# Attention with tokens on partitions in the output: four heads are divided by their sums at once and transposed back

## The chip, the cores and the metric

The kernel runs on one core of a Trainium2 chip. The metric is the device time of one execution in microseconds. The kernel before has a median of 1493.06 us over three runs (1490.69 to 1493.82).

## The reference

Two transformer blocks for 256 tokens of width 1024, in float32. The first block mixes tokens in four ways (FoX attention, a gated delta rule, HGRN and GLA) and ends in a gated feed-forward layer; the second has two attentions of eight heads (MoBA and MLA), gates, and a layer of 16384 experts. The change concerns the three attentions, all causal, with heads of 64 value columns. Each computes for a head

```
s = einsum('bhqd,bhkd->bhqk', q, k) * scale        # FoX adds c[q] - c[k]; MLA has a rotary part
s = where(k_pos <= q_pos, s, -inf)
p = softmax(s)
o = einsum('bhqk,bhkd->bhqd', p, v)
```

With 256 tokens MoBA has one block of keys, so it is plain causal attention. FoX has four heads, MoBA and MLA eight each.

## The kernel before, in words

Activations lie with features on partitions and the 256 tokens along the free axis. Weights come from HBM by SP's queue as 128x1024 float32 tiles; ScalarE copies each into a rounded `hi` (line 163, carried out in the helper at line 146) and VectorE or GpSimd subtracts to get `lo` (line 164), and a projection makes three matmuls of each pair of tiles (`dense_n`, line 314; `columns_into`, line 364; `branch`, lines 178 to 180). `prefetch` issues these for the weight after next.

The attentions share the generator `attention` (line 937). For head i, `soft` writes the scores into one PSUM bank: queries 0 to 127 against 128 keys, queries 128 to 255 against 256 keys (lines 1178 and 1179 for FoX, 1543 for MoBA, 1555 and 1556 for MLA). VectorE adds the mask and takes the maxima (lines 946 and 948), scales the maxima (line 950), ScalarE makes the exponentials and their sums, and VectorE takes the reciprocal of the sums (line 953) and scales the two parts (lines 954 and 955). One turn later the three 128x128 pieces are transposed (line 974) and ScalarE copies them to SBUF as `at_t` (`fat` in FoX). Another turn later `pv` multiplies: the values are stationary (128 keys x 64 columns), the transposed probabilities move (256 and 128 columns, lines 933 and 934), and the output has features on partitions, two heads above each other. A bank holds four heads. When the fourth is done, `after` (line 1526) has ScalarE copy the bank to `yos`, and `split` (line 182) makes the `hi` and `lo` for the output projection; FoX copies its bank to `os_` and goes on to its norm (`finish`, line 906: squares, a matmul at line 492, the reciprocal root).

Float32 matmuls show up as two passes each; a transpose is one.

The order of the work is written out by hand. Every stage is a Python generator, and the strings `TURNS1` and `TURNS2` say which of them emits its next piece (`follow`, line 387). Each engine carries out its instructions in the order of emission. A projection emits half a tile at a turn, 12 matmuls. Around the ends of the groups of four heads the order is:

- FoX: fourth product, then 24 projection matmuls with two weight splits, then the step that copies the bank and squares it, then the split of another mixer's output (`Xh` from `gatez`, `Xl`), then the norm's matmul.
- MoBA, heads 0 to 3: fourth product, scores of head 5, 24 projection matmuls with one weight split on VectorE, then the step, which goes on with the transposes of head 4.
- MoBA, heads 4 to 7: fourth product, 36 projection matmuls and other work, the scores of an MLA head, 12 projection matmuls, the step.
- MLA, heads 0 to 3: fourth product, scores of head 5, the step at once, with the transposes of head 4 behind it, 12 projection matmuls, the product of head 4.
- MLA, heads 4 to 7: fourth product, the step at once, then the output branch of MLA, the first half of whose matmuls needs heads 0 to 3 only.

PSUM has eight banks: four under the tag "m" (scores, transposes, norms), two "n" (outputs of MoBA and MLA), two "d" (projections).

Of the kernel before, what the change touches and what calls it, by code (L numbers as in the profile page):

```python
# [116 lines left out]
def _emit(ctx, tc, I, out):  # L117
# [819 lines left out]
    def attention(pool, heads, scores, scale, v, out_of, new_e, new_t, tag, after=lambda h: None,  # L937
                  names=lambda h: (), lt=1, lp=1):
        sc, pt = {}, {}

        def soft(i):
            b = bank(tag)
            scores(heads[i], b)
            e = new_e(i)
            m = pool.tile([128, 4], F32, tag="at_m", name="at_m", bufs=4)
# [4 lines left out]
            V.tensor_scalar(m[:, 0:2], m[:, 0:2], -scale, None, op0=OP.mult)  # L950
            A(e[:, 0:128], e[:, 0:128], AF.Exp, bias=m[:, 0:1], scale=scale, accum_out=m[:, 2:3])
            A(e[:, 128:384], e[:, 128:384], AF.Exp, bias=m[:, 1:2], scale=scale, accum_out=m[:, 3:4])
            V.reciprocal(m[:, 2:4], m[:, 2:4])
            V.tensor_scalar(e[:, 0:128], e[:, 0:128], m[:, 2:3], None, op0=OP.mult)
            V.tensor_scalar(e[:, 128:384], e[:, 128:384], m[:, 3:4], None, op0=OP.mult)
            sc[i] = e

        n = len(heads)
        for i in range(n + lt + lp):
            j = i - lt - lp  # L960
            if j >= 0:
                t = pt.pop(j)
                pv(out_of(heads[j]), t[:, 0:256], t[:, 256:384], lambda kt: v(kt, heads[j]))
            if i < n:
                yield from need(*names(heads[i]))
                soft(i)
            yield
            if j >= 0:
                after(heads[j])
            if 0 <= i - lt < n:  # L970
                b = bank(tag)
                e = sc.pop(i - lt)
                for z in range(3):
                    PE.transpose(b[:, z * 128:(z + 1) * 128], e[:, z * 128:(z + 1) * 128], ident)
                pt[i - lt] = new_t(i - lt)
                A(pt[i - lt], b[:, :384], AF.Copy)
                yield
# [169 lines left out]
    def fox():  # L1147
# [26 lines left out]
        def scores(h, b):  # L1174
            r_ = slice((h % 2) * 64, (h % 2) * 64 + 64)
            for w, t, n in ((b[:, 0:128], 0, 128), (b[:, 128:384], 1, 256)):
# [4 lines left out]
        o = bank()  # L1181
        ab_ = [z.rearrange("p (a b) -> p a b", a=2) for z in (mp.tile([128, 768], F32, tag="ffb", name="fae"), mp.tile([128, 768], F32, name="fat"))]
        yield from attention(tmp, range(4), scores, 1.0, lambda kt, h: vcols(kt, h * 64),
                             lambda h: head(b2(o), h), lambda i: ab_[0][:, i % 2], lambda i: ab_[1][:, i % 2], "m")
        os_ = q
        A(os_, b2(o), AF.Copy)
        yield from finish(0, os_, "fon", None, "m")

    follow([main1(), gdn(), fox(), hgrn(), gla(), gdn_gates()], TURNS1)
# [325 lines left out]
                              out_rows(3), branch("b", 3), out_rows(4), out_rows(5), out_rows(6), out_rows(7)])  # L1515

    def attend(n, scores, scale, v, names=lambda h: ()):
        o = {}

        def out_of(h):  # L1520
            g = h // 4
            if g not in o:
                o[g] = b2(bank("n"))
            return o[g][(h % 2) * 64:(h % 2) * 64 + 64, (h % 4) // 2]

        def after(h):
            if h % 4 == 3:
                g = h // 4
                os_ = btmp.tile([128, 2, 256], F32, tag="yos", name="yos")
                A(os_, o[g], AF.Copy)  # L1530
                split(os_, ya[n][0][:, 2 * g:2 * g + 2], ya[n][1][:, 2 * g:2 * g + 2])

        yield from attention(btmp, range(8), scores, scale, lambda kt, h: v[:, kt, h * 64:h * 64 + 64], out_of,
                             lambda i: btmp.tile([128, 384], F32, tag="at_e" + n, name="at_e", bufs=LAG[0] + 1),
                             lambda i: btmp.tile([128, 384], F32, tag="at_t" + n, name="at_t", bufs=LAG[1] + 1), "m", after, names, *LAG)

    def moba():
        def scores(h, b):
# [475 lines left out]
```

## Time and profile before

| what | us |
|---|---|
| median of three runs | 1493.06 |
| the profiled execution's own time | 1492.48 |
| its span, first to last instruction | 1490.5 |
| TensorE matmul busy | 1430.4 (96%) |
| VectorE busy | 1011.9 (68%) |
| ScalarE busy | 778.6 (52%) |
| GpSimd busy | 293.3 (20%) |
| mean granted TensorE clock | 0.978 of full speed |

Times in a profile count from the start of the span. PE is TensorE's matmuls and PEld its weight loads, DVE is VectorE, ACT ScalarE, POOL GpSimd, SP the engine that issues most DMAs. A row of the timeline gives the start, the time from there to the end of the last instruction merged into the row, the engine, the line, the operation, what it writes and reads, its shape (for a matmul the stationary operand first, as 128*64 for 128 rows and 64 columns, then the moving one), how many were merged, and in brackets how long the engine had been idle and what ended that. Helpers record their own line: all of ScalarE's activations stand at L146. Successive matmuls overlap, so the time of one is read from the start of the next.

### The profile page before, as it was taken

The page shows a single profiled execution, that of the slowest core. Times are in us where ns is not written, and L with a number is a line of the kernel's source. Part 1 is how long each engine was busy: PE and PEld are TensorE (multiplying, and loading weights), DVE is VectorE, ACT ScalarE, POOL GpSimd, SP SyncE. Part 2 cuts the span into 40 slices and gives each one's busy share as a digit, 9 for nine tenths or more (in the row PEclk, how much of TensorE's full clock was granted, in tenths as well). Part 3 has the DMA queues.
Part 4 walks back from the last instruction along what each step waited for, and adds up shares of the span by engine and source line. Part 5 has one row for each costly group of instructions (what it writes and reads, how often), then busy time and mean ns, then how long its engine had stood idle before and what let it go on. Part 6 is the DMA issues. An engine that isn't in the chain of part 4 may idle for free.

```text
span 1490.5 us, 27184 instructions
## 1 busy us (share of the span) xinstructions
PE 1430.4 (96%) x11076; PEld 1305.4 (88%) x11076; DVE 1011.9 (68%) x1846; ACT 778.6 (52%) x1068; POOL 293.3 (20%) x133
## 2 busy tenths in 40 slices
PE   8699989999999899999999999999999999999998
PEld 7588858999998678799999999788889999978886
DVE  5577757997786645467998887666663333666665
ACT  5633435566564446444556666444445555654444
POOL 1000000000002115332670000000037777700000
PEclk9899979999999989999999999999999999999999
DMA  6322203456654223354565455566665555566664
GB/s 235 114 85 76 68 15 116 167 192 196 185 173 155 89 93 116 111 175 151 157 190 178 156 156 157 182 193 192 194 188 168 169 170 170 171 189 194 197 194 131
DMA packets 63791, 231.42 MB, mean 155 GB/s; under 512 B 7073, under 2 KB 7602, under 8 KB 63282
## 3 DMA queue, kind: packets, MB, share of 16 engines
q1 hardware_dynamic: 62640, 226.00, 48.5%
q10 hardware_dynamic: 1026, 3.68, 0.8%
q8 instruction: 87, 1.43, 0.4%
q14 instruction: 38, 0.31, 0.1%
HBM read 228.60 MB, written 1.05 MB: 154 GB/s over the span
## 4 chain that ended last, share of the span: by engine, by line
PE 85%; DVE 8%; ACT 4%; issue 2%; DMA 0%; SPq 0%; DVEq 0%; ACTq 0%
PE bd L314 36%; PE bm L1833 8%; PE bm L1834 8%; PE bm L1832 8%; PE bn L314 6%; PE bm L348 5%; PE bn L1785 2%; DVE lo L164 2%; PE bacc L364 1%; PE bd L376 1%; ACT hi L146 1%; PE bn L933 1%; PE bm L1543 1%; PE bn L1059 1%; PE bm L1556 1%
## 5 line engine op out<-in xcount | busy, mean ns | idle before, releaser
L146 ACT ACTIVATE hi<-raw 128x1024 fp32r<-128x1024 f32 x426 | 448.1, 1057 | 180.3 <-PE bm L1833 54.3
L164 DVE TENSOR_TENSOR lo<-raw,hi 128x1024 fp32r<-128x1024 f32 x310 | 381.1, 1235 | 144.8 <-ACT hi L146 144.8
L164 POOL TENSOR_TENSOR lo<-raw,hi 128x1024 fp32r<-128x1024 f32 x116 | 284.0, 2464 | 846.6 <-ACT hi L146 557.0
L314 PE MATMUL bd<-Xh,hi 128*128 128x256 f32 x1560 | 392.6, 290 | 9.3 <-ACT hi L146 7.1
L314 PE MATMUL bd<-Xl,hi 128*128 128x256 f32 x1560 | 381.9, 283 | 0.0
L314 PEld LDWEIGHTS bd<-Xh,hi 128*128 128x128 f32 x1560 | 296.4, 190 | 14.4 <-ACT hi L146 10.2
L314 PEld LDWEIGHTS bd<-Xl,hi 128*128 128x128 f32 x1560 | 296.6, 190 | 0.8 <-issue 0.2
L314 PE MATMUL bd<-Xh,lo 128*128 128x256 f32 x1560 | 216.2, 281 | 0.0
L1832 PE MATMUL bm<-hi,eh 128*128 128x512 f32 x512 | 199.4, 389 | 2.9 <-ACT eh L146 2.9
L1833 PE MATMUL bm<-hi,el 128*128 128x512 f32 x512 | 199.4, 389 | 0.5 <-DVE el L184 0.5
L1834 PE MATMUL bm<-lo,eh 128*128 128x512 f32 x512 | 199.2, 389 | 0.0
L314 PEld LDWEIGHTS bd<-Xh,lo 128*128 128x128 f32 x1560 | 198.5, 188 | 0.0
L1770 DVE TENSOR_TENSOR oi<-iorow,IT 128x1024 f16<-128x1024 f16 x64 | 59.4, 929 | 114.3 <-PE bn L1785 112.3
L146 ACT ACTIVATE Gt<-bn 128x512 f32<-128x512 f32 x64 | 71.3, 1114 | 116.4 <-PE bn L1785 116.4
L1832 PEld LDWEIGHTS bm<-hi,eh 128*128 128x128 f32 x512 | 96.1, 188 | 23.2 <-ACT eh L146 3.3
L1833 PEld LDWEIGHTS bm<-hi,el 128*128 128x128 f32 x512 | 96.1, 188 | 20.8 <-DVE el L184 1.1
L1834 PEld LDWEIGHTS bm<-lo,eh 128*128 128x128 f32 x512 | 96.1, 188 | 20.0
L146 ACT ACTIVATE eh<-act 128x512 fp32r<-128x512 f32 x64 | 40.4, 632 | 118.8 <-DVE act L1813 118.8
L184 DVE TENSOR_TENSOR el<-act,eh 128x512 fp32r<-128x512 f32 x64 | 44.3, 692 | 49.4 <-ACT eh L146 49.4
L1772 DVE TENSOR_TENSOR jg<-eqj,GHL 128x1024 f16<-128x1024 f16 x64 | 50.7, 792 | 2.2
L314 PE MATMUL bn<-Xl,hi 128*128 128x256 f32 x192 | 47.7, 286 | 0.6 <-DVE Xl L251 0.6
L314 PE MATMUL bn<-Xh,hi 128*128 128x256 f32 x192 | 47.1, 282 | 0.0
(588 smaller groups left out, 2067.9 us busy)
## 6 DMA issues: line engine op xcount, KB each, us to landing
raw<-in_eu SPq DMA_DIRECT2D x128, 512.0 KB, 3.6
raw<-in_ev SPq DMA_DIRECT2D x128, 512.0 KB, 3.8
raw<-in_w_in SPq DMA_DIRECT2D x61, 512.0 KB, 3.6
raw<-in_w_up SPq DMA_DIRECT2D x44, 512.0 KB, 3.9
raw<-in_w_down SPq DMA_DIRECT2D x22, 512.0 KB, 4.2
raw<-in_w_out SPq DMA_DIRECT2D x16, 512.0 KB, 3.5
raw<-in_w_query SPq DMA_DIRECT2D x16, 512.0 KB, 4.0
raw<-in_w_ba SPq DMA_DIRECT2D x4, 512.0 KB, 3.5
```

The lines of the kernel that those rows point to most:

```text
L146: S.activation(o, i, f, **kw)
L164: (V if by == "v" else G).tensor_tensor(lo[:, :width], raw[:, :width], hi[:, :width].bitcast(F32), op=OP.subtract)
L184: V.tensor_tensor(lo, src, hi.bitcast(F32), op=OP.subtract)
L314: PE.matmul(o, w[:, k * 128:k * 128 + M], x[:, k], start=n == 0, stop=n == 23)
L348: PE.matmul(acc[n // 2][:, (n % 2) * 256:(n % 2) * 256 + 256], w[:, n * 128:n * 128 + 128], x, start=first and n % 2 == 0 and w is ws[0][0 ...
L364: PE.matmul(acc[n // 2][:, (n % 2) * 256:(n % 2) * 256 + 256], w[:, i * 512 + n * 128:i * 512 + n * 128 + 128], x, start=first and n % 2 = ...
L1770: V.tensor_tensor(oi, along(64), pairs(IT[:, ts], 64), op=OP.is_equal)
L1772: V.tensor_tensor(jg.rearrange("p (t i) j e -> p t i (j e)", i=2), eq.rearrange("p t j e -> p t (j e)")[:, :, None].to_broadcast([128, 8, ...
L1785: PE.matmul(p[:, t, :nj], oi[:, t].rearrange("p a b -> p (a b)"), jg[:, 2 * t + i].rearrange("p a b -> p (a b)"), start=i == 0, stop=i == 1)
L1832: PE.matmul(o, eh[:, i, ts], v[0][:, n_], start=False, stop=False, skip_group_check=True)
L1833: PE.matmul(o, el[:, i, ts], v[0][:, n_], start=False, stop=False, skip_group_check=True)
L1834: PE.matmul(o, eh[:, i, ts], v[1][:, n_], start=False, stop=last and j + i == nj - 1, skip_group_check=True)
```

## The change

The probabilities stay unscaled: line 953's reciprocal and the two scalings leave the head. The sums of four heads are gathered in one tile. The product has the transposed, unscaled probabilities stationary (128x128) and the values moving (64 columns), in three matmuls, so that the output has tokens on partitions and four heads side by side in one bank. After the fourth head, VectorE takes the reciprocal of all eight columns of sums, multiplies the bank by it into `z`, TensorE transposes `z` in four pieces into a fresh bank of tag "m", and `split` (FoX: the copy to `os_`) reads that bank directly; the copy to `yos` is gone. FoX's output bank is taken when the first product is made, and its `z` lies in the memory of the keys.

```diff
-            V.reciprocal(m[:, 2:4], m[:, 2:4])
-            V.tensor_scalar(e[:, 0:128], e[:, 0:128], m[:, 2:3], None, op0=OP.mult)
-            V.tensor_scalar(e[:, 128:384], e[:, 128:384], m[:, 3:4], None, op0=OP.mult)
+            A(e[:, 0:128], e[:, 0:128], AF.Exp, bias=m[:, 0:1], scale=scale, accum_out=tot[g][:, 0, c:c + 1])
+            A(e[:, 128:384], e[:, 128:384], AF.Exp, bias=m[:, 1:2], scale=scale, accum_out=tot[g][:, 1, c:c + 1])
             sc[i] = e
+
+        def group(g):
+
+            r = tot.pop(g)
+            V.reciprocal(r, r)
+            z = new_z()
+            V.tensor_tensor(z, out.pop(g), r[:, :, :, None].to_broadcast([128, 2, 4, 64]), op=OP.mult)
+            b = bank(tag)
+            for t in range(2):
+                for hp in range(2):
+                    PE.transpose(b[:, hp * 256 + t * 128:hp * 256 + t * 128 + 128],
+                                 z[:, t, 2 * hp:2 * hp + 2].rearrange("p a b -> p (a b)"), ident)
+            return b2(b)
...
-                t = pt.pop(j)
-                pv(out_of(heads[j]), t[:, 0:256], t[:, 256:384], lambda kt: v(kt, heads[j]))
+                p = pt.pop(j)
+                g, c = divmod(j, 4)
+                if c == 0:
+                    out[g] = bank(otag).rearrange("p (t h d) -> p t h d", t=2, h=4)
+                o = out[g]
+                PE.matmul(o[:, 0, c], p[:, 0:128], v(0, heads[j]), start=True, stop=True, skip_group_check=True)
+                PE.matmul(o[:, 1, c], p[:, 128:256], v(0, heads[j]), start=True, stop=False, skip_group_check=True)
+                PE.matmul(o[:, 1, c], p[:, 256:384], v(1, heads[j]), start=False, stop=True, skip_group_check=True)
...
-            if j >= 0:
-                after(heads[j])
+            if j >= 0 and j % 4 == 3:
+                whole(j // 4, group(j // 4))
...
-        os_ = q
-        A(os_, b2(o), AF.Copy)
+                             lambda: k.rearrange("p a (b d) -> p a b d", b=4), "m", "m",
+                             lambda g, o: A(os_, o, AF.Copy))
...
-                os_ = btmp.tile([128, 2, 256], F32, tag="yos", name="yos")
-                A(os_, o[g], AF.Copy)
-                split(os_, ya[n][0][:, 2 * g:2 * g + 2], ya[n][1][:, 2 * g:2 * g + 2])
+                             lambda: btmp.tile([128, 2, 4, 64], F32, tag="at_z", name="at_z"), "m", "n",
+                             lambda g, o: split(o, ya[n][0][:, 2 * g:2 * g + 2], ya[n][1][:, 2 * g:2 * g + 2]), names, *LAG)
```

The turns and their strings are the same.

## Rows read from the trace of the kernel before

**Rows 1.** The page: busy time and instructions by engine; the chain by engine.
```profile
PE 1430.4 (96%) x11076; PEld 1305.4 (88%) x11076; DVE 1011.9 (68%) x1846; ACT 778.6 (52%) x1068; POOL 293.3 (20%) x133
...
PE 85%; DVE 8%; ACT 4%; issue 2%; DMA 0%; SPq 0%; DVEq 0%; ACTq 0%
```

**Rows 2.** Busy time by stretch: length, PE, PEld, DVE, ACT, POOL, granted clock, DMA.
```profile
548.00:551.00 3.00, 3.00 (x9) 1.48 (x8) 1.20 (x8) 0.98 (x4) 0.00 (x0) 0.50 0.11 38
551.00:554.00 3.00, 3.00 (x7) 1.47 (x8) 0.44 (x3) 0.00 (x0) 0.00 (x0) 0.50 0.00 0
554.00:557.00 3.00, 3.00 (x15) 3.00 (x16) 1.88 (x9) 0.99 (x4) 0.00 (x0) 0.51 0.00 0
...
605.00:608.00 3.00, 3.00 (x9) 1.68 (x8) 0.58 (x4) 1.29 (x2) 2.11 (x1) 0.50 0.00 0
608.00:611.00 3.00, 3.00 (x16) 3.00 (x15) 1.55 (x7) 2.60 (x7) 0.31 (x1) 0.50 0.50 180
```

**Rows 3.** Groups by line and shape, 470 to 640 us: busy, mean ns, idle before.
```profile
L955 DVE TENSOR_SCALAR at_e<-at_e,at_m 128x256 f32<-128x256 f32 x16 | 5.6, 348 | 0.0
...
L953 DVE RECIPROCAL at_m<-at_m 128x2 f32<-128x2 f32 x16 | 2.7, 166 | 17.0 <-ACT at_e L146 17.0
...
L1458 DVE TENSOR_TENSOR gta<-bd,R 128x512 f32<-128x512 f32 x4 | 2.7, 683 | 0.0
```

**Rows 4.** Timeline, FoX: its first head, its last product and its norm.
```profile
197.16 2.08 PE L492 MATMUL bn<-hsq,cst 128*128 128x512 f32 x2
...
199.82 0.68 DVE L234 TENSOR_SCALAR f3v<-bn 128x512 f32<-128x512 f32 x1
...
233.23 0.60 ACT L146 ACTIVATE fq<-bm 128x512 f32<-128x512 f32 x1 [0.56 <-PE bm L934]
...
234.01 2.35 DVE L164 TENSOR_TENSOR lo<-raw,hi 128x1024 fp32r<-128x1024 f32 x2
...
236.07 1.02 PE L492 MATMUL bm<-hsq,cst 128*128 128x512 f32 x2
...
245.10 0.38 PE L364 MATMUL bacc<-Xl,hi 128*128 128x256 f32 x1 [1.82 <-DVE Xl L184]
```

**Rows 5.** Timeline, MLA: the product of a head and the scores after it.
```profile
583.53 0.65 PE L933 MATMUL bn<-at_t,vb 128*64 128x256 f32 x2
...
584.33 0.48 PE L1555 MATMUL bm<-kno,qno 64*128 64x128 f32 x2
...
584.74 0.48 PE L1556 MATMUL bm<-kpe,qpe 32*128 32x128 f32 x2
```

**Rows 6.** Timeline: float32 matmuls with 128x128 stationary and few moving columns.
```profile
126.03 0.28 PE L683 MATMUL bm<-g,cst 128*128 128x4 f32 x2
...
127.73 0.31 PE L717 MATMUL bm<-kept,s 128*128 128x128 f32 x1
...
725.03 2.01 PE L1627 MATMUL bm<-keys,qT 128*128 128x128 f32 x16
```

**Rows 7.** Timeline, MoBA, the step after its fourth head.
```profile
534.00 0.49 PE L974 MATMUL bm<-kept,at_e 128*128 128x128 f32 x3
534.02 1.23 DVE L164 TENSOR_TENSOR lo<-raw,hi 128x1024 fp32r<-128x1024 f32 x1 [0.20 <-ACT hi L146]
```

**Rows 8.** Timeline, MoBA, ahead of the step after its eighth head.
```profile
572.44 0.17 DVE L950 TENSOR_SCALAR at_m<-at_m 128x2 f32<-128x2 f32 x1
...
573.17 0.28 PE L314 MATMUL bd<-Xh,hi 128*128 128x256 f32 x1
```

**Rows 9.** Timeline, MLA, around the step after its fourth head.
```profile
599.74 0.55 PE L974 MATMUL bm<-kept,at_e 128*128 128x128 f32 x3
...
600.52 0.17 DVE L950 TENSOR_SCALAR at_m<-at_m 128x2 f32<-128x2 f32 x1
...
603.28 0.43 PE L933 MATMUL bn<-at_t,vb 128*64 128x256 f32 x1 [1.58 <-ACT at_t L146]
```

**Rows 10.** Timeline, MLA, the output branch after its eighth head.
```profile
631.59 0.38 PE L178 MATMUL bd<-yb,hi 128*128 128x256 f32 x1 [0.44 <-ACT yb L146]
```

More of the change, by code (lines that the diff above doesn't have):

```diff
@@ L934, in pv, with attention @@
         PE.matmul(o[:, 128:256], v(1), pt1, start=False, stop=True, skip_group_check=True)
-    def attention(pool, heads, scores, scale, v, out_of, new_e, new_t, tag, after=lambda h: None,
-                  names=lambda h: (), lt=1, lp=1):
-        sc, pt = {}, {}
+    def attention(pool, heads, scores, scale, v, new_e, new_t, new_z, tag, otag, whole, names=lambda h: (), lt=1, lp=1):
+        sc, pt, out, tot = {}, {}, {}, {}
         def soft(i):
+            g, c = divmod(i, 4)
+            if c == 0:
+                tot[g] = pool.tile([128, 2, 4], F32, tag="at_s", name="at_s", bufs=2)
             b = bank(tag)
@@ L944, in soft @@
             e = new_e(i)
-            m = pool.tile([128, 4], F32, tag="at_m", name="at_m", bufs=4)
+            m = pool.tile([128, 2], F32, tag="at_m", name="at_m", bufs=4)
             V.tensor_tensor_reduce(out=e[:, 0:128], in0=b[:, 0:128], in1=mask[:, 128:256], op0=OP.add, op1=OP.max,
@@ L961, in attention @@
             if j >= 0:
-                t = pt.pop(j)
-                pv(out_of(heads[j]), t[:, 0:256], t[:, 256:384], lambda kt: v(kt, heads[j]))
+                p = pt.pop(j)
+                g, c = divmod(j, 4)
+                if c == 0:
+                    out[g] = bank(otag).rearrange("p (t h d) -> p t h d", t=2, h=4)
[3 more added lines that the diff above has]
+                PE.matmul(o[:, 1, c], p[:, 256:384], v(1, heads[j]), start=False, stop=True, skip_group_check=True)
             if i < n:
@@ L1179, in scores @@
                 PE.matmul(w, ca[r8, ts], cb[r8, h, 0:n], start=False, stop=True)
-        o = bank()
+        os_ = q
         ab_ = [z.rearrange("p (a b) -> p a b", a=2) for z in (mp.tile([128, 768], F32, tag="ffb", name="fae"), mp.tile([128, 768], F32, name="fat"))]
         yield from attention(tmp, range(4), scores, 1.0, lambda kt, h: vcols(kt, h * 64),
-                             lambda h: head(b2(o), h), lambda i: ab_[0][:, i % 2], lambda i: ab_[1][:, i % 2], "m")
-        os_ = q
-        A(os_, b2(o), AF.Copy)
+                             lambda i: ab_[0][:, i % 2], lambda i: ab_[1][:, i % 2],
+                             lambda: k.rearrange("p a (b d) -> p a b d", b=4), "m", "m",
+                             lambda g, o: A(os_, o, AF.Copy))
         yield from finish(0, os_, "fon", None, "m")
@@ L1517, in attend @@
     def attend(n, scores, scale, v, names=lambda h: ()):
[L1518 to L1528, printed above, removed]
-                os_ = btmp.tile([128, 2, 256], F32, tag="yos", name="yos")
-                A(os_, o[g], AF.Copy)
-                split(os_, ya[n][0][:, 2 * g:2 * g + 2], ya[n][1][:, 2 * g:2 * g + 2])
-        yield from attention(btmp, range(8), scores, scale, lambda kt, h: v[:, kt, h * 64:h * 64 + 64], out_of,
+        yield from attention(btmp, range(8), scores, scale, lambda kt, h: v[:, kt, h * 64:h * 64 + 64],
                              lambda i: btmp.tile([128, 384], F32, tag="at_e" + n, name="at_e", bufs=LAG[0] + 1),
-                             lambda i: btmp.tile([128, 384], F32, tag="at_t" + n, name="at_t", bufs=LAG[1] + 1), "m", after, names, *LAG)
+                             lambda i: btmp.tile([128, 384], F32, tag="at_t" + n, name="at_t", bufs=LAG[1] + 1),
+                             lambda: btmp.tile([128, 2, 4, 64], F32, tag="at_z", name="at_z"), "m", "n",
+                             lambda g, o: split(o, ya[n][0][:, 2 * g:2 * g + 2], ya[n][1][:, 2 * g:2 * g + 2]), names, *LAG)
     def moba():
```

4 lines of the change are left out of this document (1 added, 3 removed).

## The prediction

> **What bounds the kernel now.** I read the page first, then the busy time by stretch, then the groups of the attention stretches by shape, then the timeline around each place where a group of four heads ends. TensorE is the bound: 1430 us of a 1490.5 us span, and 85% of the chain that ended last [rows 1]. So a microsecond of matrix work, or of TensorE standing still, counts nearly in full; a microsecond of VectorE counts only where TensorE waits for it. The attentions run near 193 to 245 us (FoX) and 473 to 632 us (MoBA, MLA), woven into the projections. There TensorE counts as busy 3.00 us of every 3, yet the granted clock falls to 0.50, that is 1.2 of its 2.4 GHz [rows 2]; the work in the two low stretches is scores, products and transposes, the long projections being the minority. Half speed over 548 to 557 costs some 4.5 us (1.5 + 1.5 + 1.47), over 605 to 611 some 3.0.
>
> **VectorE, removed per head.** A reciprocal (0.17 us) and two scalings (0.35 for the wide one, the narrow one no more): some 0.8 us, twenty times, 16 us in all [rows 3]. The reciprocal also holds VectorE about 1.06 us for the exponentials (17.0 us over 16 heads). I cost this gain at nothing in MoBA and MLA. What follows there in VectorE's queue is mostly a weight split `lo`, which waits for ScalarE's `hi`, and that stands behind the same exponentials; so the queue stalls on `hi` instead of on the sums. TensorE's list of waits has none of a transpose of probabilities on the scalings. If that cover is gone, at most the 16 us less what runs beside matmuls would come back; no row shows it. In FoX the chain does pass through the scalings. Their successor starts at 199.82, while its input, a matmul begun at 197.16 and 2.08 long, is there at 199.24 [rows 4]: **-0.6 us**; bounds 0 and, were both blocked heads to gain the whole 0.8, -1.6.
>
> **The products.** Before: two matmuls a head, each two passes, 64 stationary columns, 256 and 128 moving; from 583.53 to the next work at 584.33 that is 0.80 us [rows 5]. After: three matmuls, six passes, 128 stationary columns and 64 moving. No row has that shape, but two bracket it [rows 6]: with 4 moving columns 16 passes took 126.03 to 127.73, 0.106 each; with 128 moving, 16 passes lasted 2.01 in all, at most 0.126. I take 0.11, as the shape lies between them: 0.66 a head, -0.14 by twenty heads, **-2.8 us**. The low end is 0.106 (-3.3). The high end is from the scores, whose matmul with 128 moving columns took 0.41 (584.33 to 584.74) [rows 5]: 0.21 of it two loads, the rest the stream, so with half the stream 0.31 a matmul, 0.93 a head, +2.6.
>
> **The five group ends.** Each now has, in one step: the sums' reciprocal (0.17), one multiply of 128x512 out of PSUM (0.69 as the projection evictions [rows 3]), four transposes (4 x 0.11 = 0.44), then the copy or split. The multiply waits for the fourth product, and the transposes for the multiply. TensorE is in order, so everything behind stands still: projection matmuls, the next head's transposes. I place each by the order in which the instructions stand now.
>
> *FoX.* The group's step comes after 24 projection matmuls, and VectorE is in two `lo` splits until 234.01 + 2.35 = 236.36 [rows 4]. Reciprocal and multiply end near 237.2, the transposes 237.9; the copy (0.60, until now at 233.23 under those matmuls) and a square taken as long now follow, and the norm's matmul starts at 239.2 in place of 236.07. ScalarE's `Xh` of the gated output stood behind the square, so it slides too, and its `Xl` after it, ahead of the norm on VectorE: the chain loses some 3.4. Nothing absorbs it, for the end of that chain, `Xl` at 245.1, is what TensorE already waits 1.82 for: **+3.4 us**.
>
> *MoBA, first group.* The transposes would stand where a head's transposes start now, 534.00; a `lo` split ahead of the reciprocal starts at 534.02 and takes 1.23 [rows 7]. z is ready at 536.1: a stall of 2.1, plus 0.44: **+2.5**. Behind the stalled step wait ScalarE's split of the result, the next `at_t` copy, a `hi`, and on VectorE the projection's eviction; all slide by about as much as TensorE does, so no second wait follows.
>
> *MoBA, second.* VectorE ends the next head's maximum at 572.61; z at about 573.6; the 12 matmuls before the step end at 573.17 [rows 8]: 0.43 + 0.44, **+0.9**.
>
> *MLA, first.* No other work lies between scores and step: TensorE would stand from 599.74 until z, 600.69 + 0.17 + 0.69 and gaps, 601.65 [rows 9]. But today it waits 1.58 for `at_t`, since two ScalarE copies stand ahead; one is gone, and that wait is eaten. After the four transposes (0.44), the three (0.3) and 12 matmuls (1.45) the product starts at 603.9 in place of 603.28: **+0.6**.
>
> *MLA, second.* The copy (0.60, as FoX's) becomes the multiply (0.69) and the transposes with their drain (0.6); the half of the first output branch that needs no new data still covers the split. The second half, now at 631.59 after a wait of 0.44 [rows 10], starts some 0.7 later: **+0.7**.
>
> The four removed ScalarE copies count nothing beyond that. No DMA is added or moved, so SP's queue is the same, and POOL's instructions stand as before; their `lo` splits only start later with TensorE. The extra PSUM bank rotates among four, freed in each case earlier than it is asked for again: nothing, bounds 0 to +0.5 a group.
>
> **Sum.** -0.6 - 2.8 + 3.4 + 2.5 + 0.9 + 0.6 + 0.7 = +4.7 on the profiled execution, 1492.48, gives 1497.2. The median of the runs is 0.6 above that execution, so I forecast 1497.8 for the median.
>
> **Rivals.** *A, the forecast*, 0.46; alone 1495.3 to 1500.3.
>
> *B, the products cost more than the bracket* (load and stream in series, as in the scores): +5.4 over my value, 1503.2. For it: scores do so in the same stretch. Against: they use part of the rows, and both bracketing rows use the full array. 0.08.
>
> *C, the clock falls once more.* The stalls at 534 and 599 are each followed by transposes and short products; a new low stretch like that at 605 to 611 costs 3.0, one like 548 to 557 4.5: 1500.8 to 1502.3. For it: today's low stretch at 605 begins after the 1.58 wait [rows 2, 9]. Against: dense projections follow most stalls. 0.14. Of that the Trainium skill says (TensorE: Matmul & The Clock Gate, Part 4: PE-mode transpose) that transposes do not count as busy for the clock gate in the way matmuls do. By that rule the 20 added transposes lengthen each idle patch and C would be the forecast, 1500.8 in place of 1497.8. The trace neither shows nor denies it, since its low stretches mix transposes with scores and products.
>
> *D, the clock stays up.* Full-width products replace half-width ones just where the clock is low now; if both low stretches go, 7.5 is given back: 1490.3, not slower than before. It decides from the point where the clock holds through 548 to 557. For it: the products there are the only half-width work. Against: the scores, with 32 or 64 rows, remain and are longer. 0.20.
>
> *E, the stalls are covered.* If VectorE, freed of 16 us, reaches the multiplies early, what is left is transposes (+2.2), products (-2.8) and FoX's -0.6, with half of FoX's tail (+1.7): +0.5, 1493.6. Against: in each place I named the instruction in front of the reciprocal, and none of them is removed. 0.12.
>
> **Numbers.** 0.2%, about 3 us, is what a measurement of this kernel can tell from no change: faster is below 1490.1, slower above 1496.0. A gives 0.40 slower and 0.06 same; B and C 0.22 slower; D 0.09 faster and 0.11 same; E 0.10 same and 0.02 faster. So faster 0.11, same 0.27, slower 0.62. The range 1489.5 to 1503 reaches from D's lower half to the dearer C and the edge of B.
>
> **What would show it.** Right: TensorE waiting on VectorE's z for some 2 us in MoBA's first and MLA's first group and 0.4 in MoBA's second; FoX's norm matmul about 3 us later after its last product; a head's products at 0.66; MoBA's and MLA's weight splits no earlier against the exponentials. Wrong: no waits on z; products at 0.9; TensorE's clock at full through MoBA's last heads; or a low clock behind the new stalls. A gain of over 3 us would mean that VectorE's relief or the clock, which I leave out of the forecast, did the work.

## The result and the profile after

The changed kernel takes **1501.34 us** (median of 8 runs, 1499.24 to 1508.86) against 1493.01 for the kernel before (8 runs): a ratio of 1.0062, 95% interval 1.0046 to 1.0078, so 8.3 us slower. The forecast was 1497.8 within 1489.5 to 1503.0. Direction and range hold; the middle was 3.5 us short.

The profiled execution took 1505.11 (span 1503.3) at a mean granted clock of 0.969. Runs of one kernel differ in this clock and their time goes with it, so a kernel's runs are compared at one clock below.

The page of the changed kernel, against [rows 1]:

```profile
PE 1440.3 (96%) x11136; PEld 1321.6 (88%) x11136; DVE 1001.6 (67%) x1796; ACT 776.9 (52%) x1064; POOL 291.7 (19%) x133
...
PE 84%; DVE 9%; ACT 4%; issue 2%; DMA 0%; SPq 0%; DVEq 0%; ACTq 0%
```

VectorE lost 10.3 us of work, ScalarE 1.7, and TensorE is busy 9.9 us longer with 60 instructions more. By the forecast's prices the matrix work itself is 0.6 us less (2.2 of transposes, 2.8 less of products); a TensorE at 1.2 GHz is busy for longer with the same work.

TensorE's list of waits (what waited, for whom, us in total, times, longest) has the new ones, here among others that are left out:

```profile
PE bm L967 <- DVE at_z L963: 4.5, 3, 2.0
...
PE bn L980 <- ACT at_t L146: 2.6, 3, 1.3
...
PE bm L967 <- DVE fk L963: 1.7, 1, 1.7
...
PE bacc L364 <- DVE Xl L184: 1.6, 1, 1.6
...
PE bm L492 <- ACT hsq L146: 1.3, 1, 1.3
```

L967 is a group's transposes, L963 the multiply that makes `z`, L980 to L982 the products. Before the change the products waited 4.1 for `at_t`, and there was no line for z:

```profile
PE bn L933 <- ACT at_t L146: 4.1, 4, 1.6
```

The timeline at FoX's group end, from its last product on, against [rows 4]:

```profile
235.01 0.33 PE L980 MATMUL bm<-vt,fat 128*128 128x64 f32 x2
...
239.63 0.69 DVE L963 TENSOR_TENSOR fk<-bm,at_s 128x512 f32<-128x512 f32 x1
...
240.38 0.66 PE L967 MATMUL bm<-kept,fk 128*128 128x128 f32 x4 [1.71 <-DVE fk L963]
241.07 0.60 ACT L146 ACTIVATE fq<-bm 128x512 f32<-128x512 f32 x1 [5.35 <-PE bm L967]
...
242.38 2.08 PE L492 MATMUL bm<-hsq,cst 128*128 128x512 f32 x2 [1.35 <-ACT hsq L146]
```

In the kernel before the last product starts at 232.33:

```profile
232.33 0.65 PE L933 MATMUL bm<-fat,vt 128*64 128x256 f32 x2
```

The chain runs as the prediction laid it out: multiply, transposes, copy, square, norm. From the last product to the norm's matmul it is 7.37 us in place of 3.74, so the norm comes 3.6 later (forecast about 3). The norm's two matmuls take 2.08 where they took 1.02, at a granted clock of 0.50. MoBA's first group, against [rows 7]:

```profile
543.79 1.22 DVE L164 TENSOR_TENSOR lo<-raw,hi 128x1024 fp32r<-128x1024 f32 x1 [2.01 <-ACT hi L146]
544.94 0.19 DVE L961 RECIPROCAL at_s<-at_s 128x8 f32<-128x8 f32 x1
...
545.16 0.69 DVE L963 TENSOR_TENSOR at_z<-bn,at_s 128x512 f32<-128x512 f32 x1
...
545.91 1.00 PE L967 MATMUL bm<-kept,at_z 128*128 128x128 f32 x4 [1.98 <-DVE at_z L963]
```

The `lo` split in front of the reciprocal is the one named, and TensorE stands 1.98 (forecast 2.1). MLA's first group waits 1.77:

```profile
614.88 1.11 PE L967 MATMUL bm<-kept,at_z 128*128 128x128 f32 x4 [1.77 <-DVE at_z L963]
```

MoBA's second group does not wait in this profile, and 0.25 in a second profile of the changed kernel:

```profile
579.92 0.63 PE L967 MATMUL bm<-kept,at_z 128*128 128x128 f32 x4 [0.25 <-DVE at_z L963]
```

MLA's second group shows the products' price at full clock:

```profile
641.25 0.43 PE L980 MATMUL bn<-vb,at_t 128*128 128x64 f32 x2 [0.58 <-ACT at_t L146]
...
641.52 0.39 PE L981 MATMUL bn<-vb,at_t 128*128 128x64 f32 x2
...
641.74 0.39 PE L982 MATMUL bn<-vb,at_t 128*128 128x64 f32 x2
...
642.17 0.69 DVE L963 TENSOR_TENSOR at_z<-bn,at_s 128x512 f32<-128x512 f32 x1 [0.99 <-PE bn L982]
...
642.91 0.66 PE L967 MATMUL bm<-kept,at_z 128*128 128x128 f32 x4 [0.79 <-DVE at_z L963]
```

A matmul of two passes starts 0.22 after the one before it: 0.66 for three, as forecast. The prediction read the 0.80 of the kernel before from the first product to the next work; read so, a head now takes 0.58 to 0.81, most often 0.71, but the first product also starts sooner after the projection matmul ahead of it, 0.12 in place of 0.21. Together that is a gain of about 0.16 a head, near the forecast's 0.14. What differs is the clock. Busy time by stretch (length, PE, PEld, DVE, ACT, POOL, granted clock, DMA), against [rows 2]:

```profile
512.00:515.00 3.00, 1.67 (x14) 1.36 (x13) 1.26 (x3) 1.65 (x4) 1.65 (x1) 1.00 0.01 4
515.00:518.00 3.00, 3.00 (x12) 2.23 (x12) 1.14 (x6) 0.40 (x3) 0.70 (x1) 0.56 0.41 141
518.00:521.00 3.00, 2.36 (x12) 1.96 (x11) 0.00 (x0) 1.07 (x4) 0.00 (x0) 0.50 0.09 34
521.00:524.00 3.00, 3.00 (x12) 2.79 (x13) 0.00 (x0) 0.00 (x0) 0.00 (x0) 0.50 0.00 0
524.00:527.00 3.00, 3.00 (x11) 2.25 (x11) 0.81 (x5) 0.70 (x3) 0.00 (x0) 0.50 0.00 0
...
614.00:617.00 3.00, 2.12 (x10) 2.12 (x11) 1.13 (x3) 1.92 (x6) 0.00 (x0) 0.56 0.08 27
```

A low stretch of some 13 us lies in MoBA's first heads, ahead of any group end of MoBA; the kernel before has nothing like it in either of its two profiles. The short one at 614 is at MLA's first group end.

### The profile page after: what moved, and what is told of

It reads as the page before. It is cut to its first block, busy times and chain, and to the rows that moved or that the text cites. A ratio compares the mean times of both kernels' runs of the same rounds, so it can differ in the third digit from the quotient of the medians.

```text
span 1503.3 us, 27252 instructions
## 1 busy us (share of the span) xinstructions
PE 1440.3 (96%) x11136; PEld 1321.6 (88%) x11136; DVE 1001.6 (67%) x1796; ACT 776.9 (52%) x1064; POOL 291.7 (19%) x133
## 4 chain that ended last, share of the span: by engine, by line
PE 84%; DVE 9%; ACT 4%; issue 2%; DMA 0%; SPq 0%; DVEq 0%; ACTq 0%
PE bd L314 36%; PE bm L1839 8%; PE bm L1840 8%; PE bm L1838 8%; PE bn L314 6%; PE bm L348 5%; PE bn L1791 2%; DVE lo L164 2%; PE bd L376 1%; PE bacc L364 1%; ACT hi L146 1%; PE bm L1549 1%; PE bn L1078 1%; DVE s L530 1%; PE bm L1633 1%
## 5 line engine op out<-in xcount | busy, mean ns | idle before, releaser
L314 PE MATMUL bd<-Xh,hi 128*128 128x256 f32 x1560 | 396.6, 292 | 9.6 <-ACT hi L146 7.3
L314 PEld LDWEIGHTS bd<-Xl,hi 128*128 128x128 f32 x1560 | 299.8, 192 | 0.8 <-issue 0.2
L314 PE MATMUL bn<-Xl,hi 128*128 128x256 f32 x192 | 47.6, 285 | 0.6 <-DVE Xl L251 0.6
L314 PE MATMUL bn<-Xh,hi 128*128 128x256 f32 x192 | 47.2, 283 | 0.0
```

The costliest lines, as they stand in the source:

```text
L314: PE.matmul(o, w[:, k * 128:k * 128 + M], x[:, k], start=n == 0, stop=n == 23)
```

## The experiments

Two tools serve them all. **By stage**: the lengths between the first matmuls of named lines, with the sum of (1 - granted clock) x length over stretches of 3 us, the clock's loss, in brackets. It is an upper bound on what the low clock costs, since a wait is counted too. Each row is one profile.

| us | FoX's scores to L330 | MoBA's scores to keys' turn | to MLA's scores | MLA's first to last score | to L1627 |
|---|---|---|---|---|---|
| before | 59.8 (12.8) | 43.4 (1.7) | 28.7 (0.0) | 70.3 (8.5) | 67.9 (0.3) |
| before, again | 59.8 (13.0) | 43.4 (1.7) | 28.8 (0.0) | 70.2 (8.5) | 67.9 (0.1) |
| changed | 64.9 (15.3) | 48.8 (8.0) | 31.4 (2.3) | 68.4 (6.8) | 68.6 (0.0) |
| changed, again | 64.8 (14.7) | 44.5 (3.0) | 30.0 (0.5) | 69.1 (6.8) | 68.5 (0.0) |
| early multiply | 63.6 (14.6) | 48.8 (8.0) | 27.7 (0.5) | 67.5 (6.8) | 69.9 (1.9) |
| FoX old | 57.5 (9.7) | 43.1 (1.7) | 32.5 (1.7) | 69.0 (6.8) | 68.6 (0.0) |
| FoX only | 66.5 (18.3) | 48.8 (7.8) | 27.6 (0.7) | 70.2 (8.6) | 68.0 (0.3) |
| no group step | 62.4 (16.6) | 47.5 (6.5) | 27.2 (0.3) | 70.2 (10.2) | 66.7 (0.0) |
| no division | 58.5 (11.3) | 46.8 (6.4) | 27.8 (0.5) | 68.8 (6.8) | 68.0 (0.0) |
| early, FoX old | 59.4 (11.8) | 47.2 (6.2) | 27.7 (0.7) | 67.5 (6.8) | 69.0 (1.7) |
| product only | 61.7 (14.7) | 47.2 (6.2) | 27.0 (0.6) | 67.1 (6.8) | 66.9 (0.0) |
| no group step, wide | 58.4 (11.3) | 47.6 (6.4) | 27.3 (0.5) | 67.4 (6.8) | 66.9 (0.2) |
| early, wide | 62.3 (13.5) | 44.8 (3.1) | 27.7 (0.3) | 66.4 (5.1) | 69.2 (1.7) |
| early, wider still | 62.0 (11.4) | 44.0 (1.2) | 28.9 (0.5) | 65.1 (1.7) | 68.2 (0.0) |

(L1178, L330, L1543, L1402, L1555 and L1627 of the kernel before and their counterparts.)

**At one clock**: within a kernel, time falls by 0.99 us for each 0.001 of mean clock (one slope fitted to 214 runs, those of all kernels in the table but the last). Moving every run to 0.974 by that slope and averaging parts the time that is left at one clock from what the clock gives or takes. It is a reading across runs: the scatter of these means is 0.2 to 0.5 us (0.7 for the early multiply with FoX old, 0.9 for FoX old, with 6 runs), and kernels fitted alone give slopes of 0.86 to 1.39. The mean clocks scatter by 0.0003 for the kernel before and by 0.0004 to 0.0016 for the others. The runs of the experiments were made on four chips, the kernel before on each of them: there its mean clock was 0.9752 to 0.9761 and its median 1492.8 to 1493.4.

| kernel | runs | median | ratio to before, interval | mean clock | at 0.974 |
|---|---|---|---|---|---|
| before | 98 | 1493.04 | | 0.9755 | 1494.8 |
| changed | 14 | 1502.10 | 1.0062, 1.0076 | 0.9714 | 1500.9 |
| early multiply | 12 | 1498.18 | 1.0038, 1.0016 to 1.0059 | 0.9711 | 1496.1 |
| FoX old | 6 | 1501.69 | 1.0058, 1.0035 to 1.0080 | 0.9727 | 1500.0 |
| FoX only | 12 | 1496.69 | 1.0032, 1.0012 to 1.0051 | 0.9726 | 1496.9 |
| no division | 12 | 1493.24 | 1.0002, 0.9984 to 1.0021 | 0.9747 | 1494.1 |
| no group step | 12 | 1494.78 | 1.0005, 0.9991 to 1.0020 | 0.9704 | 1491.1 |
| early, FoX old | 12 | 1494.20 | 1.0016, 0.9994 to 1.0038 | 0.9732 | 1495.8 |
| product only | 12 | 1493.78 | 0.9993, 0.9978 to 1.0007 | 0.9728 | 1491.8 |
| no group step, wide | 12 | 1488.95 | 0.9973, 0.9959 to 0.9988 | 0.9749 | 1490.4 |
| early, wide | 12 | 1493.32 | 0.9992, 0.9973 to 1.0012 | 0.9768 | 1495.1 |
| early, wider still | 12 | 1490.70 | 0.9991, 0.9977 to 1.0006 | 0.9819 | 1499.7 |

### The changed kernel again

No edit.

> The changed kernel once more, profiled and timed on one chip with the three kernels that follow. Both theories: about 1.006 of the kernel before (1500 to 1502 us). The stall theory (the time lies in the waits on z and in FoX's tail) expects the same waits on z at the same places (FoX 1.7 us, MoBA's first group 2.0, MLA's first 1.8), whatever the clock does. The clock theory (half or more of the loss is TensorE at 1.2 GHz for longer in MoBA and MLA) expects the stretch from 473 to 653 us to lose some 7 us more to a low clock than the kernel before does, in a run with another mean clock too; if that sum comes down to that of the kernel before, the profiled run of 1505 was only a run with a low clock and the clock theory loses its main row.

The median is 1502.66, a ratio of 1.0076 (1.0052 to 1.0100). The waits on z are 4.8 us, four of them, and 1.7 in FoX, at the same places. The profiled run (1500.42, clock 0.974) loses 3.0 in place of 8.0 in MoBA's first stage: that low stretch differs between two runs of one kernel. From MoBA's first scores to MLA's last the loss adds up to 10.3, as in the kernel before (10.2), where the first profile had 17.1. By the condition that the expectation set, the clock theory loses its main row: in this profile only FoX's stage loses more than before (14.7 against 12.8 and 13.0). Between the kernels 6.1 us stand at one clock (1500.9 against 1494.8), and a mean clock 0.004 lower, over all 14 runs, is worth 4 more. Neither theory alone has it.

### The multiply right behind the fourth product

```diff
-        def group(g):
-
+        zs = {}
+
+        def divide(g):
             r = tot.pop(g)
             V.reciprocal(r, r)
-            z = new_z()
-            V.tensor_tensor(z, out.pop(g), r[:, :, :, None].to_broadcast([128, 2, 4, 64]), op=OP.mult)
+            zs[g] = new_z()
+            V.tensor_tensor(zs[g], out.pop(g), r[:, :, :, None].to_broadcast([128, 2, 4, 64]), op=OP.mult)
+
+        def group(g):
+            z = zs.pop(g)
...
+                if c == 3:
+                    divide(g)
```

> The reciprocal and the multiply of a group are issued right behind its fourth product, ahead of the weight split and the next head's maximum in VectorE's queue; only the four transposes stay a turn later. Stall theory: the waits of the transposes on z fall from 1.7, 2.0, 1.8 and 0.8 us to under 0.4 each, FoX's norm matmul comes some 1.7 us earlier, and the time falls by 4 to 6 us against the changed kernel, to about 1496 (1.002 of the kernel before). Clock theory, with low stretches that belong to the short products and transposes and not to the stalls: the waits go just the same, but the stretch from 473 to 653 us still loses 7 us more to the low clock than before, and the time falls by 2 us at most, to 1499. If the low stretches are set off by the stalls, they go with them and the time is at or below 1493.

The median is 1498.18. TensorE's waits:

```profile
PE bn L984 <- ACT at_t L146: 3.0, 4, 1.3
...
PE bm L971 <- DVE at_z L964: 0.8, 1, 0.8
...
PE bm L971 <- DVE fk L964: 0.6, 1, 0.6
```

Waits on z fall from 6.5 (4.8 + 1.7) to 1.4, by 5.1 us; the time at one clock falls by 4.8. So the stalls cost close to their full length. The fall of 4.5 from 1502.66, on the same chip, is what the stall theory said; that the time stops at 1498 and not at its 1496 goes with the mean clock, which stays at 0.9711: it is not the stalls that lower it. The waits that are left are over the expected 0.4: 0.8 in MLA's second group, where nothing lies between product and transposes, and 0.6 in FoX.

### FoX old, and FoX alone

Each half of the change: the old function for FoX's call, or for MoBA's and MLA's.

```diff
-        yield from attention(tmp, range(4), scores, 1.0, lambda kt, h: vcols(kt, h * 64),
+        yield from attention_old(tmp, range(4), scores, 1.0, lambda kt, h: vcols(kt, h * 64),
...
-        yield from attention(btmp, range(8), scores, scale, lambda kt, h: v[:, kt, h * 64:h * 64 + 64],
+        yield from attention_old(btmp, range(8), scores, scale, lambda kt, h: v[:, kt, h * 64:h * 64 + 64], out_of,
```

> FoX's attention as before the change, MoBA's and MLA's as after it. By the forecast's terms FoX is worth +2.2 us (3.4 of tail, -0.6 of relief, -0.56 of its products), so that this kernel should be 2.2 faster than the changed one; by the profiled run of the changed kernel FoX's stage was worth +5.1. Stall theory: 3 to 5 us faster than the changed kernel, 1.003 of the kernel before. Clock theory: 1 to 2 us faster, since the low stretches of MoBA and MLA stay, 1.005.

> FoX's attention as after the change, MoBA's and MLA's as before it; the other half of the sum. By the forecast's terms +2.2 us over the kernel before (1.0015); by the profiled run of the changed kernel +5.1 (1.0034). Stall theory: 3 to 5 over the kernel before, and the two halves add up to the 8.3 us of the whole. Clock theory: 1 to 2 over it, and the clock in MoBA's and MLA's stretch as in the kernel before.

FoX alone stands 2.1 us over the kernel before at one clock, where the forecast's terms gave 2.2. MoBA and MLA alone stand 5.2 over it (4.0 as the changed kernel less FoX alone), where the terms gave 2.5. The two halves make 7.3, over the 6.1 of the whole but within the scatter of the means. FoX old was expected under the changed kernel by 2.2 us (the forecast's terms), 3 to 5 (the stall theory) or 1 to 2 (the clock theory), and is 1.0 under it. The clock theory also had FoX alone at the clock of the kernel before in MoBA and MLA; its profile loses 17.1 there against 10.2. Both halves have a mean clock about 0.003 lower, which for FoX old, with its 6 runs, is less than twice the scatter. FoX alone has the 8-us low stretch in MoBA's first stage although its MoBA is the old one, and the kernel with FoX old and MoBA new lacks it; it isn't MoBA's own instructions that set it.

### No division

```diff
-            V.reciprocal(m[:, 2:4], m[:, 2:4])
-            V.tensor_scalar(e[:, 0:128], e[:, 0:128], m[:, 2:3], None, op0=OP.mult)
-            V.tensor_scalar(e[:, 128:384], e[:, 128:384], m[:, 3:4], None, op0=OP.mult)
```

> The kernel before with the reciprocal and the two scalings of the probabilities left out (the division by the sums is left out of the computation): VectorE's relief alone, 16 us of VectorE, with nothing added. The forecast's terms: 0 in MoBA and MLA and 0.6 us off in FoX, bounds 0 and 1.6, so 0.9996 of the kernel before (0.9989 to 1). The rival, relief that reaches TensorE at each head: 0.2 us or more for each of 20 heads, 4 us, 0.9973 or lower. MoBA's and MLA's stretch from the first scores to the last should keep its length less the clock's loss within 0.5 us by the forecast.

The ratio is 1.0002, and the time at one clock 0.7 less: relieving VectorE of 16 us gives nothing that can be told from zero. The forecast's 0.6 fits, the rival's 4 us does not. The expectation on lengths fails: from MoBA's first scores to MLA's last, less the clock's loss, it is 129.7 against 132.2. Two waits of TensorE are shorter in this profile: the 1.3 for `qno` is missing, as in FoX alone, and that for `at_t` is 3.4 in place of 4.1. The row of this kernel also loses 6.4 in MoBA's first stage, with the old products and no new step.

### No group step

```diff
         def group(g):
-
-            r = tot.pop(g)
...
-            return b2(b)
+            return out.pop(g).rearrange("p t h d -> p t (h d)")
```

> The changed kernel without the group's reciprocal, multiply and transposes; the copy or split reads the product's bank as it is (the division and the transposition of the outputs are left out of the computation). What is left of the change is VectorE's relief, the three-matmul products and four copies less. The forecast's terms: -0.6 - 2.8 and nothing for the group ends: 1489.6, 0.9977 of the kernel before; against the changed kernel at the same mean clock 6.3 + 3.4 = some 9 to 10 us less. Rival, products at 0.93 us a head: 1495, 1.0014. On the clock: if full-width products hold it up, the stretch from MLA's first scores to its last loses less than the 8.5 us that the kernel before loses there, at or under the 6.8 of the changed kernel.

At one clock this kernel is 3.7 us below the kernel before (forecast 3.4): the price of the products is right, and rival B falls. Yet the median is 1.7 *above* it, and by the interval the two can't be told apart: the mean clock, 0.9704, is the lowest of all kernels, with no stall on z and not one added transpose. MLA's stage loses 10.2, more than the 8.5 before, so the full-width products did not hold the clock up there, as the expectation asked. The stretches of FoX's heads (200 to 240) and of MoBA and MLA (473 to 640), in this kernel:

```profile
200.00:240.00 40.00, 39.85 (x270) 32.71 (x270) 20.06 (x45) 16.75 (x37) 0.00 (x0) 0.66 0.07 27
473.00:640.00 167.00, 159.13 (x1056) 141.63 (x1056) 75.64 (x160) 80.83 (x158) 49.80 (x21) 0.90 0.36 107
```

and in the kernel before, profiled again on the same chip:

```profile
200.00:240.00 40.00, 38.77 (x287) 30.89 (x287) 24.92 (x57) 18.58 (x40) 0.00 (x0) 0.80 0.18 51
473.00:640.00 167.00, 155.41 (x1025) 132.45 (x1024) 88.37 (x209) 83.31 (x162) 53.05 (x21) 0.94 0.35 108
```

The granted clock is the column before the last two: 0.66 against 0.80, 0.90 against 0.94. That asks for a new theory, tried in the next runs: the product's new form, not what was built around it, lowers the clock.

### Early multiply with the old FoX, and the kernel before again

The two edits above together; and no edit.

> FoX's attention as before; MoBA's and MLA's as changed, with the reciprocal and multiply right behind the fourth product. By the terms that are left: products -2.2 (16 heads), four groups of transposes +1.8, MLA's second group +0.7, one wait on z of 0.8: +1.1, that is 1494 at the clock of the kernel before (1.0007), and 1.5 to 2 under the early multiply with the new FoX. If it is the clock that costs, not stalls and FoX's tail, it stays at 1.003 or above. Below 0.998 of the kernel before it would be a version worth keeping; neither theory expects that.

> The kernel before, for one more profile on the same chip. If the low clock over 512 to 530 us, which the profiles of the early multiply and of FoX alone show (8 us lost from MoBA's first scores to the turn of the keys, in place of 1.7) although MoBA's own code differs between them, comes and goes from run to run, this profile may show it too; if it never shows in a kernel with the old FoX, it hangs on when FoX lets MoBA start. FoX's stage should lose 10 to 13 us to the clock, against 14.6 to 18.3 in the four profiles with the new FoX.

With most of the waits gone and FoX old, the kernel is 1.0 us over the kernel before at one clock; the terms gave 1.1. The median, 1494.20, can't be told from 1493.04. FoX's stage loses 11.8 in it, and in the second profile of the kernel before 13.0; MoBA's first stage loses 6.2 with FoX old too, so the low stretch there is not tied to the new FoX, as the expectation had it. The kernel before shows 1.7 both times.

### The product alone

The kernel without the group's step, with the division put back at each head:

```diff
+            V.reciprocal(tot[g][:, :, c], tot[g][:, :, c])
+            V.tensor_scalar(e[:, 0:128], e[:, 0:128], tot[g][:, 0, c:c + 1], None, op0=OP.mult)
+            V.tensor_scalar(e[:, 128:384], e[:, 128:384], tot[g][:, 1, c:c + 1], None, op0=OP.mult)
             sc[i] = e
```

> The kernel before with its per-head reciprocal and scalings kept, and only the products in the new form; the group's transposes are left out (the outputs stay untransposed), and the copy or split reads the product's bank. The run without the group's step had, at one mean clock of 0.974, 1491.0 against 1494.5 for the kernel before, and a mean clock of 0.970 against 0.9755 that gave some 5 us back. Theory now: the product form does both, so this kernel has a mean clock of 0.970 to 0.972, 1491 to 1491.5 at 0.974, and ends 1 to 2 us over the kernel before (1.000 to 1.001). Rival: the clock falls because VectorE's work per head is gone and TensorE runs in another rhythm; then this kernel keeps 0.975 and comes out at 1490, 0.998.

The median is 1493.78, the time at one clock 3.0 less than before, the mean clock 0.9728: below the 0.9755 of the kernel before, above the 0.9704 without the division, and a little above the expected 0.970 to 0.972. The clock falls with VectorE's work in place, so the rival, by which it would have kept 0.975, fails as the whole explanation; the absence of that work seems to take another 0.002, which is at the edge of what these runs tell. Most of the gain of 3.0 is given back: the ratio is 0.9993. Beside the products' form, this kernel also lacks the four copies to `yos`.

### Wider products

Each product takes the next head's values too, 128 moving columns; the next head's product then overwrites what is not wanted.

```diff
-                PE.matmul(o[:, 0, c], p[:, 0:128], v(0, heads[j]), start=True, stop=True, skip_group_check=True)
+                w = min(c + 2, 4)
+                PE.matmul(o[:, 0, c:w].rearrange("p h d -> p (h d)"), p[:, 0:128], v(0, heads[j], w - c), start=True, stop=True, skip_group_check=True)
...
```

> The run without the group's step, but each product takes the values of two heads as its moving side, 128 columns in place of 64; the half that is not wanted is overwritten by the next head's product, the last head of a group takes 64 (the division and the transposition of the outputs are left out as there). Cost by the bracket of the forecast, 0.126 a pass at most in place of 0.11: at most 0.1 us a head, 1.5 us in all; serial streams would add 0.16 a head at full clock, 2.4. If the clock falls for the form of the product, the wider one raises the mean clock from 0.970 towards 0.975 and this kernel comes out 2 to 4 us below the run without the group's step; if the clock hangs on something else, it stays at 0.970 and the kernel is 0 to 2 us slower than that run.

> The early multiply (1498.2, mean clock 0.971) with the same two-head moving side; it computes all that the reference asks. If the wider product holds the clock up: 1494 to 1496, no slower than 1.002 of the kernel before. If not: 1498 to 1500. Below the kernel before it can come only if the clock gains over 5 us, which neither theory expects.

Against the same kernels with 64 columns, the one without the group's step falls from 1494.78 to **1488.95** at a clock of 0.9749 in place of 0.9704, the early multiply from 1498.18 to **1493.32** at 0.9768 in place of 0.9711. The wider pass costs next to nothing: at one clock both are 0.7 to 1.0 *below* the narrow ones, and in the timeline a head's products still start 0.22 apart:

```profile
619.12 0.38 PE L971 MATMUL bn<-vb,at_t 128*128 128x128 f32 x2
619.34 0.39 PE L972 MATMUL bn<-vb,at_t 128*128 128x128 f32 x2
619.56 0.39 PE L973 MATMUL bn<-vb,at_t 128*128 128x128 f32 x2
```

A head whose products are followed by scores mostly takes 0.76 from its first product to them in place of 0.71; 0.05 for each of 15 heads would be less than 1 us.

The stretches of the kernel without the group's step, wide:

```profile
200.00:240.00 40.00, 39.07 (x311) 32.42 (x311) 24.33 (x50) 19.76 (x41) 0.00 (x0) 0.84 0.18 54
473.00:640.00 167.00, 157.85 (x1073) 139.84 (x1073) 80.36 (x165) 81.20 (x158) 49.88 (x20) 0.92 0.36 108
```

The granted clock is 0.84 in place of 0.66 over FoX's heads. One profile speaks against reading single profiles too closely: the early, wide one has 0.70 there, with FoX 3 us later in the span; its mean over 12 runs is higher all the same.

Then the early multiply with all values up to the group's last head (256, 192, 128 and 64 columns):

```diff
-                w = min(c + 2, 4)
+                w = 4
```

> As the early multiply with the wider products, but each product takes the values of all heads from its own to the group's last: 256, 192, 128 and 64 moving columns (224 pass columns a group more). It computes all that the reference asks. If the wider product costs no time as long as its stationary load is as long (the 128-column pass cost none that the times at one clock show), the time at a mean clock of 0.974 stays at 1495.3; if wider products go on holding the clock up, the mean clock rises above 0.977 and the time comes to 1490 to 1492, a version at or under the kernel before. If the gain is used up at 128 columns, 1493 to 1494; if 256 columns take longer than their load, up to 4 us more, 1497.

The median is 1490.70 at a mean clock of 0.9819 (0.979 to 0.984), the highest of all: 10.6 us under the changed kernel's first median, 7.5 under the early multiply, and not to be told from the kernel before (0.9991, 0.9977 to 1.0006). The passes do cost more now, so the first expectation fails; a head with 192 columns:

```profile
568.94 0.49 PE L985 MATMUL bn<-vb,at_t 128*128 128x192 f32 x2
569.27 0.49 PE L986 MATMUL bn<-vb,at_t 128*128 128x192 f32 x2
569.59 0.49 PE L987 MATMUL bn<-vb,at_t 128*128 128x192 f32 x2
...
570.01 0.48 PE L1568 MATMUL bm<-kno,qno 64*128 64x128 f32 x2
```

and the same head in the early multiply with 64 columns:

```profile
567.70 0.33 PE L984 MATMUL bn<-vb,at_t 128*128 128x64 f32 x2
567.86 0.39 PE L985 MATMUL bn<-vb,at_t 128*128 128x64 f32 x2
568.09 0.39 PE L986 MATMUL bn<-vb,at_t 128*128 128x64 f32 x2
568.40 0.49 PE L1567 MATMUL bm<-kno,qno 64*128 64x128 f32 x2
```

From its first product to the scores that is 1.07 in place of 0.70. At one clock the kernel is some 3.6 us slower than the early multiply (1499.7 is carried beyond its own clocks), and it ends 7.5 faster, with the granted clock at its upper level of 2.4 GHz for more of the time:

```profile
200.00:240.00 40.00, 37.56 (x280) 29.77 (x281) 22.99 (x49) 16.66 (x37) 0.00 (x0) 0.83 0.16 47
473.00:640.00 167.00, 157.50 (x1107) 139.93 (x1106) 83.12 (x172) 82.42 (x161) 52.48 (x21) 0.98 0.38 111
```

and in the early multiply:

```profile
473.00:640.00 167.00, 158.80 (x1054) 141.02 (x1053) 76.98 (x166) 80.27 (x157) 50.00 (x21) 0.90 0.35 107
```

It is 0.98 over MoBA and MLA, against 0.94 in both profiles of the kernel before, 0.90 in the early multiply's, and 0.90 and 0.94 in the two of the changed kernel. No kernel here that does all of the work beats the one before by more than can be told.

## Why the prediction was right, and where it was short

**VectorE's relief** (0, and -0.6 in FoX): this held, with -0.7 at one clock when the division is left out.

**The products** (-2.8): this held. Three matmuls start 0.66 apart in all at full clock; the kernel is 3.0 us shorter at one clock for the product alone, and 3.7 with the relief where the sum had 3.4. The bracket by full-array rows was the right one and rival B's, by the scores, the wrong one.

**FoX's tail** (+3.4): this held in sum. FoX alone is +2.1 at one clock where its three terms make +2.2. The wait on z, 1.71, stands where VectorE's two `lo` splits were named; not named was TensorE's wait of 1.35 for the square, which is part of the same chain.

**MoBA and MLA** (+2.5, +0.9, +0.6, +0.7, less 2.2): the waits are the ones named. MoBA's first is 1.98 (forecast 2.1); its second is none in the first profile, where the matmuls ahead of it ran at 1.2 GHz and covered it, and 0.25 in the second (0.43); MLA's first is 1.77 (1.9), with the 1.58 for `at_t` gone as said; MLA's second is 0.79 ahead of the transposes, and the stage to L1627 0.6 to 0.7 longer (0.7). Summed over the list of waits from MoBA's scores to L1627 in the second profile: z +4.8, `at_t` 2.6 in place of 4.1, `yb` -0.4, makes +2.9 (a wait of 1.3 for `qno` is left aside, for FoX alone lacks it too); with 1.8 of transposes and 2.2 less of products, +2.5, the forecast's own sum. The time at one clock says 4.0 to 5.2, and the early multiply with the old FoX (1.0 against 1.1) and the 4.8 us that the early multiply saves agree with the waits. The missing 1.5 to 2.7 are two to three times the scatter of these means; what they are was not settled, and no list of waits has them.

**The clock** (0): this is the step that failed, and with 4 us the largest part of what the forecast's middle lacks; the direction and the range held without it. The forecast let the low stretches stand as they were and gave rival C 0.14, rival D 0.20. The mean clock fell from 0.9755 to 0.9714, at 0.99 us for 0.001 some 4 us, which is about C's price of 3.0 to 4.5. With 6.1 at one clock that makes 10; the medians of the two comparisons are 8.3 and 9.7 apart. But C's cause was wrong. It put the new low stretch down to the stalls at the group ends; taking most of the stalls away left the clock at 0.9711, and taking stalls and transposes away left it at 0.9704. D's reason was wrong in sign: it held that full-width products would keep the clock up, and the product alone lowered it to 0.9728. What raised it again was making each product move more columns, at next to no cost up to 128: 0.9749 and 0.9768, and 0.9819 at up to 256.

What is shown is that these kernels have a higher mean clock when each product moves more columns: from 64 to 128 is one edit with all else kept, made twice, and the mean clock rose by 0.0045 and 0.0057. Narrow and wide kernels were timed on different chips, but in the kernel before these differ by 0.0009 at most. That the same thing lowered the clock from the kernel before, which moves 256 and 128 columns in each product, is argued from there and not shown: the kernel with the product alone also changes the stationary width, the number of matmuls and the copies. By stage it can be seen in FoX only. FoX's stage loses 9.7 to 13.0 us in the five profiles with FoX's old products, 14.6 to 18.3 in the six with the new ones at 64 columns, and 11.3 to 13.5 in the three with wider ones. From MoBA's first scores to MLA's last there is no such border: 10.2 to 17.1 in the four profiles with the old products there, 10.2 to 17.1 in the seven with the new ones at 64 columns, then 13.7, 8.5 and 3.4 with wider ones. From MLA's first to its last score, which holds both low stretches of [rows 2], the changed kernel loses even less than before, 6.8 against 8.5. How the chip arrives at its decision isn't shown.

The Trainium skill (TensorE: Matmul & The Clock Gate, Part 4: PE-mode transpose) says that transposes do not count as busy for the clock gate as matmuls do, and the prediction had C as the forecast by that rule. The time came out near C, but the kernel with none of the 20 added transposes has the lowest clock, so the added transposes are not what lowered it; the rule itself these runs neither show nor deny.

## What to carry to other kernels

Where TensorE is the bound and its granted clock is already dipping, a reshaped matmul has two prices: its duration at full clock, which rows of like shape give well, and what it does to the clock of the stretch around it, which they don't give. Compare kernels at one mean clock and compare the clocks; most of 3 us gained in matmul time went that way here, and widening the moving side at next to no cost brought some 5 back. An operation that TensorE waits for belongs right behind its last input in the other engine's queue: moving the multiply ahead of a weight split or of the next head's maximum saved 4.8 us at one clock with no work changed.

## What was not expected of the hardware

- Float32 products with 128x128 stationary follow each other no later with 128 moving columns than with 64: 0.22 for the two passes of a matmul either way. With 192 it is 0.33.
- The kernel whose products take longer (0.37 us more for a head with 192 columns) was 7.5 us faster than the same kernel with 64-column ones; the granted clock over MoBA and MLA was 0.98 in place of 0.90, in one profile of each.
- The low stretch in MoBA's first stage lost 8.0 us in one profile of the changed kernel and 3.0 in another, and appears (6.2 to 8.0) in kernels whose code there differs, two of them with the old products of MoBA. In two profiles of the kernel before it lost 1.7. What sets it remains open.
- 16 us less of VectorE work in the attentions, at 68% busy, moved the time by nothing that can be measured.
